# A two-layer hybrid decoder trunk on one core: the modulation weights laid transposed, their column sums formed along the row on VectorE, and the first norm's statistics with tokens on partitions

## The chip, the cores and the metric

The kernel runs on one core of a Trainium2 chip. It is one program with five engines that each work through their own list of instructions in order: PE (TensorE, matrix products; its weight loads are listed apart as PEld), DVE (VectorE), ACT (ScalarE), POOL (GpSimd) and SP (SyncE, which issues nearly all DMAs here). Engines wait for each other by semaphores. SBUF is the memory on the chip, 128 partitions wide, PSUM holds what PE writes, and weights come from HBM by DMA.

The metric is the device time of one execution in microseconds (us). The traces are of one profiled execution each, which has its own time; the other runs have no trace.

## What is computed

The input is x (512 tokens of 1024 features) and one condition vector c (1024). Two layers follow one another; each has three sub-layers, a feed-forward half step, a token mixing, and another feed-forward half step. Before each the state is normed and modulated by a shift, a scale and a gate that come from c:

```python
def rms_norm(x, gain):
    y = xf * lax.rsqrt(jnp.mean(xf * xf, axis=-1, keepdims=True) + EPS)
    return (y * gain).astype(x.dtype)

def swiglu(x, w_in, w_out):
    gate, up = jnp.split(x @ w_in, 2, axis=-1)
    return (jax.nn.silu(gate) * up) @ w_out

c_act = jax.nn.silu(c)
for l in range(DEPTH):                                    # 2
    mod = (c_act @ w_ada[l] + b_ada[l]).reshape(B, 9, 1024)
    sh1, sc1, gt1, sh2, sc2, gt2, sh3, sc3, gt3 = ...
    hn = rms_norm(h, g_ffn1[l]) * (1.0 + sc1) + sh1
    h = h + 0.5 * (1.0 + gt1) * swiglu(hn, w_ffn1_in[l], w_ffn1_out[l])
    hn = rms_norm(h, g_mix[l]) * (1.0 + sc2) + sh2
    ...                                                   # attention, RWKV-7, short convolution
    h = h + (1.0 + gt2) * mixed
    hn = rms_norm(h, g_ffn2[l]) * (1.0 + sc3) + sh3
    h = h + 0.5 * (1.0 + gt3) * swiglu(hn, w_ffn2_in[l], w_ffn2_out[l])
```

The change is about `mod`: one vector of 1024 times a matrix of 1024 x 9216 in each layer, all in float32 (37.7 MB of weights a layer, each used once). The matrices of the feed-forward steps are 1024 x 5632 and 2816 x 1024.

## The kernel before

**State and products.** The state h lies with features on partitions: eight tiles of 128 features x 512 tokens. All large products are made of three fast matmuls in a reduced format: weights and activations are each split into a high and a low part (`split`: ACT casts the high part, L89, DVE subtracts it for the low part, L90), and `mm3` issues high x high (L84), high x low (L85) and low x high (L86) into one PSUM tile `ps_mm`. One tile of a feed-forward input product is 8 pieces of the inner dimension x 3 = 24 matmuls of 128x512.

**Weights.** `load_w` brings 128x1024 floats (512 KB) into `wraw` (two buffers) by a DMA on SP and splits them into `wH` and `wL` (four buffers each), so weights can be ready up to four tiles ahead. The order of instructions on each engine is fixed when the program is built; a scheduler may pull instructions ahead of where the code issues them, as far as their buffers are free.

**Modulation in the body.** `todo` lists the half vectors (layer, one of nine, half) of 512 outputs. A step (`ada_step`) forms one of them: eight DMAs of 256 KB bring 128 rows each of `w_ada` (`wada`, three buffers), and DVE multiplies each by the silu of c on its partition and adds them up (`ada_add`: first L145, then seven times L147), giving a 128x512 tile whose columns must still be summed over the partitions. That sum is closed in the next step (`ada_close`): the tile is split into `ada_h` and `ada_l` (L89, L90), two matmuls with a matrix of ones (L174, L175) put the total on every partition, and DVE multiplies by an identity (L177), reduces along the row (L179) and adds the bias (L164). The half vector then lies as four columns of `mod`, features on partitions, which is how the norms use it. 32 of these steps run in three feed-forward stages: 13 in the first of layer 0 (`ffn1`), 7 in the second of layer 0 (`ffn2`), 12 in the first of layer 1. `ada_until` makes sure that what the next sub-layer needs is done.

**The start (`begin`).** The first shift and scale can't be hidden behind anything, so they are made in four groups, each for two tiles of 128 features. The DMAs on SP are, in order: c, the eight tiles of x, the parameters `par`, 2 x 1 MB of modulation weights for group 0 (`wada`), two first weight tiles (`wfirst`), group 1, two more weight tiles, groups 2 and 3, then the constants `con`. For each group DVE sums five of the eight row blocks (`sums_vec`), PE takes three in plain float32 matmuls with one output row (`sums_ten`, L892), and one more matmul with ones joins both (`sums_end`, L895); ACT copies the row out (L897), four tiny matmuls lay it onto partitions (`modulate`, L903), and DVE adds bias and gain (L905, L906). Meanwhile ACT squares x (L207, L210), DVE adds the squares (L211), one matmul with ones gives the sum of squares of each token on all partitions (L931), ACT takes the root (L933), and DVE the reciprocal of the 128x512 tile (L934). `normed` then multiplies h by it (L910), modulates on ACT (L912) and splits. The first four weight tiles are consumed group by group, so PE works on a group as soon as its two normed tiles are there. 72 matmuls of ones (L925) run before.

**Between stages.** While the last output tile of a stage is still being computed, in two halves of 256 tokens, `then` prepares the next norm by halves: `stats` (sum of squares L224, Sqrt on ACT L226, reciprocal on DVE L227) and `apply` (DVE L234, ACT L235, DVE L236). ACT keeps one set of function tables at a time; going from Silu to Sqrt and back loads a table.

Of the kernel before, what the change touches and what calls it, by code (L numbers as in the profile page):

```python
# [14 lines left out]
P = 128  # L15
# [38 lines left out]
def trunk_kernel(ctx, tc, ins, out, layers=L, phases=("ffn1", "mix", "ffn2")):  # L54
# [85 lines left out]
    mod = {}  # L140

    def ada_add(acc, w, k, first):
        c = cact[:, k : k + 1]
        if first:
            ts(acc, w, c, None, ALU.mult)  # L145
        else:
            stt(acc, w, c, acc, ALU.mult, ALU.add)  # L147

    def ada_sum(pool, l, i, hf):

        src = ins["w_ada"][l].rearrange("(k p) n -> p k n", p=P)
        n0 = i * D + hf * 512
# [7 lines left out]
    def ada_put(l, i, hf, v):  # L160
# [3 lines left out]
        tt(mod[l, i][:, hf * 4 : hf * 4 + 4], v, prm(l, "b_ada")[:, c0 : c0 + 4], ALU.add)  # L164

    todo = [(l, i, hf) for l in range(layers) for i in range(9) for hf in range(2)]
    open_ = []

    def ada_close():
        if open_:  # L170
            key, aH, aL = open_.pop()
            pt = psum([P, 4, P], "ps_ada")
            f = pt.rearrange("p a b -> p (a b)")
            mm(f, ones_r, aH, start=True, stop=False)  # L174
            mm(f, ones_r, aL, start=False, stop=True)  # L175
# [6 lines left out]
    def ada_step(pool):  # L182
        ada_close()
        if todo:
            key = todo.pop(0)
            acc = ada_sum(pool, *key)
            aH = pool.tile([P, T], F32R, name="ada_h", tag="ada", bufs=2)
            aL = pool.tile([P, T], F32R, name="ada_l", tag="ada", bufs=2)
            split(aH, aL, acc)
            open_.append((key, aH, aL))  # L190

    def ada_until(pool, l, i):
        while todo and todo[0] <= (l, i, 1):
            ada_step(pool)
        if open_ and open_[0][0] <= (l, i, 1):
            ada_close()
# [78 lines left out]
    def ffn(l, w_in, w_out, hn, im, ss, ada, need, then, first=None):  # L275
        with tc.tile_pool(name="act", bufs=2 * NF) as ap_:
            xs = []
            tiles = (t for t in projector([w_in[l, j, g] for j in range(NF) for g in range(2)], hn, BANKS[:3], first) if t is not None)
            for j in range(NF):
# [7 lines left out]
                if j in ada:  # L287
                    ada_step(ap_)
            ada_until(ap_, l, im + 2)
# [8 lines left out]
            for i in range(KD - 1):  # L298
# [5 lines left out]
                if NF + i in ada:  # L304
                    ada_step(ap_)
            last = list(pieces(KD - 1))
            ada_until(ap_, *need)
            ada_close()
# [542 lines left out]
    def begin(pool):  # L851
        hn = [tuple(hnp.tile([P, T], F32R, name=n, tag="hn") for n in ("hnH", "hnL")) for _ in range(KD)]
        m0 = const.tile([P, 2, KD], F32, name="mod0_01")
        for i in range(2):
            mod[0, i] = m0[:, i]
            for hf in range(2):
                todo.remove((0, i, hf))
        bias = prm(0, "b_ada")[:, : 2 * KD].rearrange("p (i k) -> p i k", k=KD)
        gm = small_.tile([P, KD], F32, name="gmod", tag="gmod")
        wa, wf, ws = {}, [], []  # L860

        def fetch(m):
            for k0 in (0, 4):
                w = pool.tile([P, 4, 512], F32, name="wada", tag="wada", bufs=8)
                nc.sync.dma_start(w, ins["wa0"][m, :, k0 : k0 + 4])
                for k in range(4):
                    wa[m, k0 + k] = w[:, k]
# [12 lines left out]
        VEC, TEN = (0, 1, 2, 4, 5), (3, 6, 7)  # L880
        acc, row = {}, {}

        def sums_vec(m):
            acc[m] = pool.tile([P, T], F32, name="ada_acc", tag="ada_acc", bufs=2)
            for k in VEC:
                ada_add(acc[m], wa[m, k], k, k == VEC[0])

        def sums_ten(m, ks):
            if m not in row:
                row[m] = psum([1, T], "ps_row")  # L890
            for k in ks:
                mm(row[m], cact[:, k : k + 1], wa[m, k], start=k == TEN[0], stop=False)  # L892

        def sums_end(m):
            mm(row[m], ones[:, :1], acc[m], start=False, stop=True)  # L895
            r = pool.tile([1, T], F32, name="ada_row", tag="ada_row", bufs=2)
            nc.scalar.copy(r, row[m])  # L897
            row[m] = r

        def modulate(m):  # L900
            pt = psum([P, 2, 2], "ps_ada")
            for n in range(4):
                mm(pt[:, n // 2, n % 2 : n % 2 + 1], row[m][:, n * P : (n + 1) * P], ones[:1, :1], start=True, stop=True)  # L903
# [173 lines left out]
```

## Time and profile before

| | us |
|---|---|
| three runs | 2064.97, 2067.78, 2068.11 |
| their median | 2067.78 |
| the profiled execution | 2066.95 |
| its span, first to last instruction | 2065.2 |
| mean granted TensorE clock in it | 0.995 of full |

The page of the profile also says what was moved: 252.31 MB of DMA, among it 256 transfers of 256 KB for `wada` in the body, 8 of 1 MB at the start, and 280 `wraw` transfers of 512 KB.

How to read the lines: a row of the page or of a view that groups instructions has the source line, the engine, the operation, output<-inputs, shapes, the count, then "| busy us, mean ns | idle time of the engine just before them, and what ended it". A row of the timeline has the start and the duration in us, the engine, the line and the operation; neighbours of the same kind are drawn together with their count, and in brackets stands how long the engine had been idle and what it waited for ("<-"). Matmuls overlap in the pipeline, so their rate is read from the distance of their starts, not from their duration. SPq rows are DMA issues, and their duration includes waiting for a buffer.

### The profile page before, as it was taken

Reading aid. Unit: us, or ns where it says so; the run is one execution under the profiler, and the core shown is the slowest. Engines: PE = TensorE matmul, PEld = TensorE weight load, DVE = VectorE, ACT = ScalarE, POOL = GpSimd, SP = SyncE. Lnnn points to the kernel's source line nnn. Section 1 sums busy time; section 2 is a strip of 40 time slices with the busy share of each in tenths; the row PEclk is TensorE's granted clock in tenths of the full one; section 3 lists DMA queues with packets and bytes.
Section 4 is the critical chain, followed back from the end, with each engine's and each line's share of the span. In section 5 each row is a group of like instructions: output and inputs, shape, how many; then the busy total and the mean of one; then the engine's idle time right before and its main releaser. Section 6 shows DMA issues by size and latency. Waiting matters only on the chain.

```text
span 2065.2 us, 27744 instructions
## 1 busy us (share of the span) xinstructions
PE 2031.5 (98%) x11194; PEld 1651.0 (80%) x11194; DVE 1164.7 (56%) x1833; ACT 672.2 (33%) x1044; POOL 3.9 (0%) x16
## 2 busy tenths in 40 slices
PE   9999999999999999999999999999999999999999
PEld 5788888886677888888888888888767778888888
DVE  6656665567875834554374666555577664333321
ACT  4423322246322432232243223223553233323211
POOL 0000000000000000000000000000000000000000
PEclk9999999999999999999999999999999999999999
DMA  6556555331222534453344666532212123333332
GB/s 277 189 154 193 184 170 182 102 95 31 57 63 72 173 103 135 141 160 117 112 130 144 190 194 185 176 120 72 82 41 62 54 72 90 94 100 94 100 110 67
DMA packets 102705, 252.31 MB, mean 122 GB/s; under 512 B 23216, under 2 KB 24112, under 8 KB 101552
## 3 DMA queue, kind: packets, MB, share of 16 engines
q1 hardware_dynamic: 102576, 250.53, 39.0%
q8 instruction: 88, 1.44, 0.3%
q14 instruction: 41, 0.34, 0.0%
HBM read 247.08 MB, written 3.41 MB: 121 GB/s over the span
## 4 chain that ended last, share of the span: by engine, by line
PE 88%; DVE 8%; ACT 2%; issue 1%; DMA 1%; SPq 0%; DVEq 0%; ACTq 0%
PE ps_mm L84 27%; PE ps_mm L85 26%; PE ps_mm L86 26%; DVE wL L90 1%; PE ps_av L777 1%; PE ps_sc L731 1%; PE ps_warm L925 1%; PE ps_c L537 1%; DVE rn L506 1%; DVE iP L505 1%; DVE rstd L227 1%; PE ps_row L892 0%; ACT wH L89 0%; PE ps_ada L174 0%; DVE inv L565 0%
## 5 line engine op out<-in xcount | busy, mean ns | idle before, releaser
L84 PE MATMUL ps_mm<-hnH,wH 128*128 128x512 f32 (+1 forms) x1848 | 697.2, 381 | 15.1 <-ACT hnH L235 12.5
L85 PE MATMUL ps_mm<-hnL,wH 128*128 128x512 f32 (+1 forms) x1848 | 702.4, 381 | 0.2
L86 PE MATMUL ps_mm<-hnH,wL 128*128 128x512 f32 (+1 forms) x1848 | 698.1, 379 | 1.1 <-DVE wL L90 1.1
L89 ACT CAST wH<-wraw 128x1024 fp32r<-128x1024 f32 (+1 forms) x328 | 334.4, 1021 | 1079.3 <-PE ps_mm L85 702.8
L90 DVE TENSOR_TENSOR wL<-wraw,wH 128x1024 fp32r<-128x1024 f32 (+1 forms) x328 | 387.2, 1181 | 400.5 <-ACT wH L89 392.7
L84 PEld LDWEIGHTS ps_mm<-hnH,wH 128*128 128x128 f32 x1848 | 347.1, 190 | 89.0 <-ACT hnH L235 15.2
L85 PEld LDWEIGHTS ps_mm<-hnL,wH 128*128 128x128 f32 x1848 | 350.5, 190 | 70.7 <-issue 5.1
L86 PEld LDWEIGHTS ps_mm<-hnH,wL 128*128 128x128 f32 x1848 | 350.4, 190 | 69.2 <-issue 4.8
L84 PE MATMUL ps_mm<-actH,wH 128*128 128x512 f32 (+1 forms) x792 | 290.1, 366 | 0.0
L86 PE MATMUL ps_mm<-actH,wL 128*128 128x512 f32 (+1 forms) x792 | 289.7, 366 | 0.0
L85 PE MATMUL ps_mm<-actL,wH 128*128 128x512 f32 (+1 forms) x792 | 289.6, 366 | 0.0
L147 DVE SCALAR_TENSOR_TENSOR ada_acc<-wada,cact,ada_acc 128x512 f32<-128x512 f32 x240 | 179.7, 749 | 37.9 <-DMA wada<-in_w_ada 32.2
L283 DVE TENSOR_TENSOR silu<-silu,ps_mm 128x512 f32<-128x512 f32 x88 | 60.3, 687 | 213.6 <-PE ps_mm L86 208.5
L85 PEld LDWEIGHTS ps_mm<-actL,wH 128*128 128x128 f32 x792 | 149.4, 189 | 24.6
L84 PEld LDWEIGHTS ps_mm<-actH,wH 128*128 128x128 f32 x792 | 149.4, 189 | 24.4
L86 PEld LDWEIGHTS ps_mm<-actH,wL 128*128 128x128 f32 x792 | 149.4, 189 | 24.2
L272 DVE SCALAR_TENSOR_TENSOR h<-ps_mm,cg,h 128x512 f32<-128x512 f32 (+1 forms) x36 | 24.9, 691 | 83.7 <-PE ps_mm L86 83.7
L90 DVE TENSOR_TENSOR actL<-silu,actH 128x512 fp32r<-128x512 f32 x88 | 60.1, 683 | 0.0
L89 ACT CAST actH<-silu 128x512 fp32r<-128x512 f32 x88 | 54.5, 620 | 5.1 <-DVE silu L283 5.1
L282 ACT ACTIVATE silu<-ps_mm 128x512 f32<-128x512 f32 x88 | 51.2, 586 | 2.0 <-PE ps_mm L86 2.0
L235 ACT ACTIVATE hnH<-hn_t,mod 128x256 fp32r<-128x256 f32 x80 | 36.3, 501 | 37.5 <-DVE hn_t L234 37.4
L210 ACT ACTIVATE sq<-h 128x512 f32<-128x512 f32 (+1 forms) x49 | 27.4, 567 | 32.5 <-DVE h L272 28.9
(289 smaller groups left out, 1531.5 us busy)
## 6 DMA issues: line engine op xcount, KB each, us to landing
wada<-in_w_ada SPq DMA_DIRECT2D x256, 256.0 KB
wraw<-in_w2i SPq DMA_DIRECT2D x88, 512.0 KB
wraw<-in_w1i SPq DMA_DIRECT2D x84, 512.0 KB
wraw<-in_wmi SPq DMA_DIRECT2D x40, 512.0 KB
wraw<-in_w1o SPq DMA_DIRECT2D x32, 512.0 KB
wraw<-in_w2o SPq DMA_DIRECT2D x32, 512.0 KB
wada<-in_wa SPq DMA_DIRECT2D x8, 1024.0 KB
wraw<-in_w1o SPq DMA_DIRECT2D x16, 384.0 KB
```

Of the source, the lines that this page charges most:

```text
L84: mm(acc, wH, xH, start=start, stop=False)
L85: mm(acc, wH, xL, start=False, stop=False)
L86: mm(acc, wL, xH, start=False, stop=stop)
L89: nc.scalar.copy(hi, src)
L90: nc.vector.tensor_sub(lo, src, hi.bitcast(F32))
L147: stt(acc, w, c, acc, ALU.mult, ALU.add)
L210: act(sq[:, sl], h[i][:, sl], AF.Square)
L227: nc.vector.reciprocal(r, r)
L235: act(a, t, AF.Identity, bias=sh)
L272: stt(h[i][:, sl], pt, gate[:, i : i + 1], h[i][:, sl], ALU.mult, ALU.add)
L282: act(s, pg, AF.Silu)
L283: tt(s, s, pu, ALU.mult)
```

## The change

**In the body.** The weights lie transposed: a row of `wadaT` has on partition p all 1024 inputs of output p. With silu(c) copied onto every partition (`crep`, 128x1024), one DVE instruction multiplies a 128x1024 weight tile by it and writes the sum along the row to one column of `mod`, through the accumulator output (`ada_dot`); the product overwrites the weights. A step is now four DMAs of 512 KB (two buffers), four such dots and one bias addition. The split, the two matmuls, the masking product and the reduction are gone, and with them `ada_close`. `crep` is loaded and its Silu taken again in each feed-forward stage that still has steps to run, out of that stage's own pool (three times).

**At the start.** `crep` is fetched ahead of the modulation weights, and the constants' first 128 columns (the identity) behind those of group 0. A group's weights hold two columns of scale, one of shift, transposed, and the second shift column in the old orientation: DVE forms the first three by dots, PE the fourth by eight matmuls with one column. The statistics are made with tokens on partitions: four matmuls with one output column each, Sqrt and reciprocal on a 128x4 tile, and four matmuls with the identity, whose stationary operand is the broadcast column, put rstd back over all partitions, into PSUM. The warm-up has 36 matmuls instead of 72. The rest of `con` is fetched after group 3.

In the scheduled order of the changed program, DVE has two dots behind each weight tile from the start of a feed-forward stage, and SP two `wada` transfers behind each `wraw`, until the stage's steps are used up.

```diff
-    def ada_add(acc, w, k, first):
...
-    def ada_sum(pool, l, i, hf):
-        acc = pool.tile([P, T], F32, name="ada_acc", tag="ada_acc", bufs=1)
-        for k in range(KD):
-            w = pool.tile([P, 512], F32, name="wada", tag="wada", bufs=3)
-            nc.sync.dma_start(w, src[:, k, n0 : n0 + 512])
-            ada_add(acc, w, k, k == 0)
-        return acc
...
-    def ada_close():
-        if open_:
-            key, aH, aL = open_.pop()
-            pt = psum([P, 4, P], "ps_ada")
-            f = pt.rearrange("p a b -> p (a b)")
-            mm(f, ones_r, aH, start=True, stop=False)
-            mm(f, ones_r, aL, start=False, stop=True)
-            d = E("ada_d").rearrange("p (a b) -> p a b", b=P)
-            tt(d, pt, rep("ident", 4), ALU.mult)
-            red = small_.tile([P, 4], F32, name="ada_red", tag="ada_red")
-            nc.vector.tensor_reduce(red, d, AXL.X, ALU.add)
-            ada_put(*key, red)
...
+    todo = [(l, i, hf) for l in range(layers) for i in range(9) for hf in range(2)][4:]
+
+    def ada_dot(out_, w, crep):
+        stt(w, w, 1.0, crep, ALU.mult, ALU.mult, accum_out=out_)
+
+    def ada_crep(pool):
+        c = pool.tile([P, D], F32, name="crep", tag="crep", bufs=1)
+        nc.sync.dma_start(c, ins["crep"])
+        act(c, c, AF.Silu)
+        return c
+
+    def ada_step(pool, crep):
+        if not todo:
+            return
+        l, i, hf = todo.pop(0)
         if (l, i) not in mod:
             mod[l, i] = const.tile([P, KD], F32, name=f"mod{l}_{i}")
+        for k in range(4 * hf, 4 * hf + 4):
+            w = pool.tile([P, D], F32, name="wada", tag="wada", bufs=2)
+            nc.sync.dma_start(w, ins["wadaT"][l, i, k])
+            ada_dot(mod[l, i][:, k : k + 1], w, crep)
+        m = mod[l, i][:, 4 * hf : 4 * hf + 4]
         c0 = i * 8 + hf * 4
+        tt(m, m, prm(l, "b_ada")[:, c0 : c0 + 4], ALU.add)
...
     def ffn(l, w_in, w_out, hn, im, ss, ada, need, then, first=None):
             xs = []
+            crep = ada_crep(ap_) if todo else None
...
     def begin(pool):
...
+            for n in (0, 2):
+                w = pool.tile([P, 2, D], F32, name="wada", tag="wada", bufs=8)
+                nc.sync.dma_start(w, ins["wa0"][m, :, n : n + 2])
...
+        def scales(m):
+            for n in range(2):
+                k = slice(2 * m + n, 2 * m + n + 1)
+                ada_dot(col["sc"][:, k], wa[m, n], crep)
+                stt(col["gm0"][:, k], col["sc"][:, k], g1[:, k], col["gb"][:, k], ALU.mult, ALU.add)
+
+        def shifts(m):
+            k0, k1 = (slice(2 * m + n, 2 * m + n + 1) for n in range(2))
+            ada_dot(col["sh"][:, k0], wa[m, 2], crep)
+            tt(col["sh0"][:, k0], col["sh"][:, k0], bsh[:, k0], ALU.add)
+            pt = psum([P, 1], "ps_ada")
+            for k in range(KD):
+                mm(pt, wa[m, 3][:, k * P : (k + 1) * P], cact[:, k : k + 1], start=k == 0, stop=k == KD - 1)
+            tt(col["sh0"][:, k1], pt, bsh[:, k1], ALU.add)
...
+        crep = ada_crep(pool)
         fetch(0)
+        nc.sync.dma_start(con[:, :P], ins["con"][:, :P])
         fetch_w()
         fetch_w()
         fetch(1)
...
-        for _ in range(72):
+        for _ in range(36):
             mm(pw, ones_r, ones_r, start=True, stop=True)
...
-        pt = psum([P, T], "ps_ss")
-        mm(pt, ones, ss, start=True, stop=True)
-        rstd = pool.tile([P, T], F32, name="rstd0", tag="rstd0")
-        act(rstd, pt, AF.Sqrt, bias=vals["eps"], scale=1.0 / D)
-        nc.vector.reciprocal(rstd, rstd)
-        sums_ten(0, TEN)
-        sums_end(0)
-        modulate(0)
+        pt = psum([P, NB], "ps_ss")
+        for b in range(NB):
+            mm(pt[:, b : b + 1], ss[:, b * P : (b + 1) * P], ones[:, :1], start=True, stop=True)
+        r = pool.tile([P, NB], F32, name="rstd_t", tag="rstd_t")
+        act(r, pt, AF.Sqrt, bias=vals["eps"], scale=1.0 / D)
+        nc.vector.reciprocal(r, r)
+        rstd = psum([P, T], "ps_rstd", "r0")
+        for b in range(NB):
+            mm(rstd[:, b * P : (b + 1) * P], r[:, b : b + 1].to_broadcast([P, P]), cst("ident"), start=True, stop=True)
+        scales(0)
+        shifts(0)
...
             for g, (n, k) in enumerate(groups):
                 mm3(pts[n], ws[n], k, hn[k], ALL, k == 0, k == KD - 1)
-                if m < 3:
-                    if g == 0:
-                        sums_vec(m + 1)
-                        sums_ten(m + 1, TEN[:1])
...
+                if m < 3 and g == 1:
+                    scales(m + 1)
+                    shifts(m + 1)
+                    if m == 0:
+                        split_w(2)
+                        split_w(3)
+                    normed(2 * m + 2)
+                    normed(2 * m + 3)
```

More of the change, by code (lines that the diff above doesn't have):

```diff
@@ L304, in ffn @@
                 if NF + i in ada:
-                    ada_step(ap_)
+                    ada_step(ap_, crep)
             last = list(pieces(KD - 1))
-            ada_until(ap_, *need)
-            ada_close()
+            ada_until(ap_, crep, *need)
             half = then()
@@ L878, in split_w @@
             ws.append(pair)
[L880 to L903, printed above, removed]
-            ks = slice(2 * m, 2 * m + 2)
-            tt(m0[:, :, ks], pt, bias[:, :, ks], ALU.add)
-            stt(gm[:, ks], m0[:, 1, ks], 1.0, prm(0, "g1")[:, ks], ALU.add, ALU.mult)
+        def scales(m):
[11 more added lines that the diff above has]
+            tt(col["sh0"][:, k1], pt, bsh[:, k1], ALU.add)
         def normed(k):
```

71 lines of the change are left out of this document (16 added, 55 removed).

## The prediction

> **What bounds the kernel now.** I read first the busy times and the chain of waits of the page, then windows cut where the stages begin.
>
> ```profile
> PE 2031.5 (98%) x11194; PEld 1651.0 (80%) x11194; DVE 1164.7 (56%) x1833; ACT 672.2 (33%) x1044; POOL 3.9 (0%) x16
> PE 88%; DVE 8%; ACT 2%; issue 1%; DMA 1%; SPq 0%; DVEq 0%; ACTq 0%
> ```
>
> ```profile
> 0.00:64.00 64.00, 58.71 (x219) 36.20 (x220) 38.06 (x64) 26.73 (x39) 0.21 (x4) 1.00 0.60 235
> 64.00:406.00 342.00, 342.00 (x1541) 283.99 (x1540) 208.63 (x283) 101.90 (x131) 0.00 (x0) 1.00 0.56 175
> 680.00:694.00 14.00, 11.81 (x79) 11.24 (x80) 13.46 (x27) 6.11 (x14) 0.00 (x0) 0.88 0.32 103
> 694.00:1043.00 349.00, 349.00 (x1608) 291.68 (x1607) 167.47 (x218) 100.81 (x130) 0.00 (x0) 1.00 0.43 132
> 1043.00:1066.00 23.00, 20.12 (x146) 18.87 (x145) 19.63 (x37) 11.58 (x21) 0.00 (x0) 0.95 0.43 138
> 1066.00:1419.00 353.00, 353.00 (x1625) 294.92 (x1624) 203.23 (x275) 102.71 (x134) 0.00 (x0) 1.00 0.52 161
> ```
>
> In a window row stand the stretch, its length, then PE, weight loads, DVE, ACT and POOL, each busy us (x instructions), the granted clock, the DMA share and GB/s. In three stretches, 64 to 406, 694 to 1043 and 1066 to 1419, PE has no gap at all: they are the three FFN stages in which the 32 modulation steps run. There a matmul taken away is time taken away, whatever DVE does, as long as DVE (203 to 209 of about 350 us) and the weight loads stay in front. Only the start (0 to 64) and the short changes of stage are set by something else.
>
> **PE work removed.** Each step closes with two 128x512 matmuls, which the new code doesn't have.
>
> ```profile
> L174 PE MATMUL ps_ada<-ada_h,ones_r x32: 404/404/505, 121.8 to 1407.0; 128*128 128x512 f32 x32
> L175 PE MATMUL ps_ada<-ada_l,ones_r x32: 402/402/442, 122.1 to 1407.3; 128*128 128x512 f32 x32
> ```
>
> ```profile
> 65.62 0.39 PE L84 MATMUL ps_mm<-hnH,wH 128*128 128x512 f32 x1
> ...
> 69.93 0.39 PE L86 MATMUL ps_mm<-hnH,wL 128*128 128x512 f32 x1
> ```
>
> Records last 0.40 us but overlap: these two rows are the first and last of 20 in a row, 19 starts in 4.31 us, 0.227 us each. 64 x 0.227 = **14.5 us**, all between 121 and 1408 us, in the saturated stretches. At most it would be 64 x 0.28 us = 18 if a matmul with another weight source cost half a step more; at least 12 if a few fell into gaps.
>
> **The new VectorE work: does it still hide?** Eight passes over 128x512, a split, a masking product and a reduction per step become four fused dots over 128x1024.
>
> ```profile
> L90 DVE TENSOR_TENSOR wL<-wraw,wH 128x1024 fp32r<-128x1024 f32 x280 | 341.4, 1220 | 298.3 <-ACT wH L89 290.5
> L147 DVE SCALAR_TENSOR_TENSOR ada_acc<-wada,cact,ada_acc 128x512 f32<-128x512 f32 x240 | 179.7, 749 | 37.9 <-DMA wada<-in_w_ada 32.2 <-DMA wada<-in_wa 0.5 <-DVE ada_acc L147 0.2
> L90 DVE TENSOR_TENSOR actL<-silu,actH 128x512 fp32r<-128x512 f32 x88 | 60.1, 683 | 0.0
> L234 DVE SCALAR_TENSOR_TENSOR hn_t<-h,gmod,rstd 128x256 f32<-128x256 f32 x80 | 35.1, 477 | 0.0
> ```
>
> ```profile
> L748 ACT ACTIVATION_READ_ACCUMULATOR Sc<-Sc,mx,rq x64: 185/187/191, 464.7 to 1532.0; 128x1 f32 x64
> ```
>
> The operation with three inputs grows by (749 - 477)/256 = 1.06 ns an element, so 1024 elements take 1.29 us. The dot also reads out its accumulator, which no DVE row shows; the nearest is ScalarE's, 0.187 us. Bounds: 1.29 (readout free) and 1.69 (two 512-wide passes and that readout). I take 1.40, nearer to the one-instruction row.
>
> The Trainium skill, "Vector Engine (DVE) Microarchitecture Reference", section "Points that are easy to get wrong", speaks against the change: this instruction with two sources in SBUF that aren't bf16 runs at half throughput, both read ports being used and none left for accumulator readback. The 1.06 ns of this trace, without an accumulator, isn't half of anything the trace shows; with one, no row tells. By that page it would be the rival "slow dot" below.
>
> In the scheduled order of the changed program the steps have moved forward: from the start of an FFN stage, two dots follow each weight tile on DVE and two modulation DMAs each weight DMA on SP. PE needs 24 x 0.227 = 5.45 us a tile, 10.9 us for two. DVE's load for two: 2 x 1.22 (low parts) + 0.68 (activation's) + 0.69 (silu product, the same form) + 0.15 + 4 x 1.40 = 9.6 us. It fits up to a dot of about 1.7 us. The transfers: with two buffers, two dots per tile need one landing, one dot and some 0.1 us.
>
> ```profile
> 94.65 1.05 ACT L89 CAST wH<-wraw 128x1024 fp32r<-128x1024 f32 x1 [2.80 <-PE ps_mm L85]
> ```
>
> ```profile
> 1049.41 0.33 SPq L246 DMA_DIRECT2D wraw<-in_w1i  x1
> ...
> 1053.06 1.05 ACT L89 CAST wH<-wraw 128x1024 fp32r<-128x1024 f32 x1 [0.36 <-DMA wraw<-in_w1i]
> ```
>
> A 512 KB transfer took 3.65 us from issue to use, so the loop is 3.65 + 1.40 + 0.1 = 5.15 us, under 5.45. And ACT's casts wait for PE to free a weight buffer, not for data: with four buffers about three tiles (16 us) are ready ahead, so a loop of up to 5.45 + 16/26 = 6.1 us over the 26 tiles of 13 steps would still hide. Price here: 0.
>
> **The start.**
>
> ```profile
> 2.38 15.62 PE L925 MATMUL ps_warm<-ones_r 128*128 128x128 f32 x72 [2.38 <-ACT ones_r L113]
> 10.41 0.69 DVE L211 TENSOR_TENSOR ss<-ss,sq 128x512 f32<-128x512 f32 x1
> 12.30 0.49 DVE L145 TENSOR_SCALAR ada_acc<-wada,cact 128x512 f32<-128x512 f32 x1 [1.19 <-DMA wada<-in_wa]
> 14.82 1.54 DVE L147 SCALAR_TENSOR_TENSOR ada_acc<-wada,cact,ada_acc 128x512 f32<-128x512 f32 x2 [0.46 <-DMA wada<-in_wa]
> 16.02 1.04 ACT L89 CAST wH<-wfirst 128x1024 fp32r<-128x1024 f32 x1 [6.00 <-DMA wfirst<-in_w1i]
> 18.31 1.28 ACT L933 ACT_TABLE_LOAD   x1
> 20.56 0.13 PEld L892 LDWEIGHTS ps_row<-wada,cact 128*1 128x1 f32 x1 [0.72 <-issue]
> 20.57 3.35 DVE L934 RECIPROCAL rstd<-rstd 128x512 f32<-128x512 f32 x1 [1.02 <-ACT rstd L933]
> 21.41 0.13 PEld L892 LDWEIGHTS ps_row<-wada,cact 128*1 128x1 f32 x1 [0.73 <-issue]
> ...
> 26.82 0.08 PEld L892 LDWEIGHTS ps_row<-wada,cact 128*1 128x1 f32 x1 [0.35 <-issue]
> 27.18 0.15 DVE L906 SCALAR_TENSOR_TENSOR gmod<-mod,par 128x2 f32<-128x2 f32 x1
> 27.25 0.08 PEld L892 LDWEIGHTS ps_row<-wada,cact 128*1 128x1 f32 x1 [0.34 <-issue]
> 27.43 0.81 ACT L912 ACTIVATE hn_t<-z,mod,gmod 128x512 f32<-128x512 f32 x1 [2.06 <-DVE gmod L906]
> 29.08 0.61 ACT L89 CAST hnH<-hn_t 128x512 fp32r<-128x512 f32 x1
> 29.75 0.96 PE L84 MATMUL ps_mm<-hnH,wH 128*128 128x512 f32 x3 [0.62 <-ACT hnH L89]
> ...
> 61.82 1.21 PE L84 MATMUL ps_mm<-hnH,wH 128*128 128x512 f32 x4 [0.93 <-ACT hnH L89]
> ```
>
> The last of the four groups of the first stage starts at 61.82 us; from there PE is full. What sets that instant after the change? Of data, 1 MB arrives in 14.82 - 12.30 = 2.5 us, 512 KB in 1.2. The replicated condition goes ahead, so it lands near 11 and the first megabytes near 13.4 and 16. Half of the warm-up ends at 10.2 (2.38 + 7.8), the squares' sum at 11.1: the statistics no longer wait for the warm-up's end at 18. They cost four small matmuls, a table load (1.28) and a reciprocal on four columns; then ACT loads the Silu table again (1.28) and applies it to 128x1024 (1.05), which frees the dots at about 15.9. First group: three dots (4.2) and four small operations (0.15 each), to 20.7; the product with rstd (0.68), modulation (0.81), another cast on ACT (1.05) and its own cast (0.61): first matmul at about 24 instead of 29.75. From there DVE is the bound. A group is 4.2 + 0.6 + 2 x 0.68 + 2 x 0.68 = 7.5 us, and the four first weight tiles add 4.9. So the dots of groups two, three and four end near 31, 41 and 49 (weights and normed tiles of the group before lie between them), the last operands are cast at about 52, and the last group starts there: 61.8 - 52.1 = **9.7 us** gained. With 12 dots in the chain it is 11 at a dot of 1.29 and 6.2 at 1.69. The shifts' eight one-column matmuls a group, each at most the 0.43 us between the last 512-wide row sums shown, take 3.4 us beside DVE's dots.
>
> **The changes of stage.** The replicated vector is loaded and activated again in three FFN stages, and dots stand among the norms.
>
> ```profile
> 676.47 0.74 DVE L147 SCALAR_TENSOR_TENSOR ada_acc<-wada,cact,ada_acc 128x512 f32<-128x512 f32 x1
> 677.40 1.75 DVE L227 RECIPROCAL rstd<-rstd 128x256 f32<-128x256 f32 x1 [0.20 <-ACT rstd L226]
> 680.45 0.62 PE L84 MATMUL ps_mm<-hnH,wH 128*128 128x256 f32 x3 [1.62 <-ACT hnH L235]
> ```
>
> Here PE waits for a normed tile behind the reciprocal. In the new order two dots (2.8) stand where one pass (0.74) stood: **+2.1 us** (0 if they run before the statistics arrive; 4.1 if the second pair shows too). The matching place at 1043 to 1066 gets one dot ahead of the second half's norm and, on ACT, a Silu table load, the Silu and a Sqrt table load between the casts: 1.40 + 1.28 of the 5.0 us show, I take **+2.6** (0 to 5). In the first FFN stage the load of the vector waits for the last normed tile of the start, and ACT's Silu stands ahead of a weight cast; three tiles are ready by then: 0.
>
> **Sum**, against the profiled run's 2066.95 us (span 2065.2 and 1.75 around it; 0.8 under the median): 2066.95 - 14.5 - 9.7 + 2.1 + 2.6 = **2047.4 us**. With the bounds: 2066.95 - 18 - 11 = 2038, and 2066.95 - 12 - 6.2 + 9.1 = 2058.
>
> **Rivals.**
>
> *Cold start.* Weight loads of the row sums follow each other by 0.85 us (20.56, 21.41) and later by 0.43 (26.82, 27.25): PE began at half speed, and 72 short warm-up matmuls hadn't changed that; only the dense 512-wide ones did. The new start has half the warm-up, and one-column matmuls instead of those. If the clock stays down through the first groups, 24 matmuls take 24 x 2 x 0.227 = 10.9 us, more than DVE's 7.5: the last group starts at 24 + 3 x 10.9 = 56.7 and itself takes up to 5.4 more. Nothing is left of the start's gain: 2066.95 - 14.5 + 4.7 = **2057**. Against it: before the change the pace doubled between 21.41 and 26.82, after few matmuls. The Trainium skill, "TensorE: Matmul & The Clock Gate", section "What's actually happening", puts the release after one busy window of about 3.4 us and the throttle after an idle one, so waits on DVE between groups could throttle it again; the two paces agree with its half rate.
>
> *The gain is hidden or spent elsewhere*: the start ends as before, because a chain through ACT (two table loads, the Silu, casts) takes the place of DVE's, and the stage changes cost their upper 9.1: 2066.95 - 14.5 + 9.1 = **2061.5**. For it: ACT has three switches of table at the start. Against: ACT was busy 27 of 64 us.
>
> *Slow dot*, on the other side: the fused dot with accumulator runs at half rate, 2 x 1.06 x 1.024 + 0.2 = 2.4 us. DVE's two-tile load becomes 13.6 against 10.9 us. Over 13, 7 and 12 steps the lag is 35, 19 and 32 us, less 16 of lead each: 19 + 3 + 16 = 38 us of starved PE, and the start's 12 dots add 12: 2047.4 + 50 = **2097**. It decides from a dot of about 1.7 us, and the lead is used up at 2.05. For it: no row shows a DVE accumulator.
>
> *Starved queue*: SP holds weight loads behind modulation loads that wait for a buffer. At a loop of 7 us the lag is 26 x 1.55 - 16 = 24, 24 x 1.55 - 16 = 21 and 14 x 1.55 - 16 = 6: **2098**. It decides at 6.1; the measured 3.65 us landing would have to be 5.5. Bandwidth doesn't speak for it: 1.5 MB in 5.45 us is 275 GB/s, and the start moves 1 MB in 2.5 us.
>
> **How the numbers follow.** Forecast 0.56, cold start 0.18, hidden or spent 0.11, slow dot 0.10, starved queue 0.05. Forecast's own range 2038 to 2058. The slower 0.15 can be left out, with little at the low end: 2038 to 2064. About 0.2% (4 us) is what a measurement here tells from no change. Faster holds the forecast, the cold start and half of hidden: 0.79; same, the rest of hidden: 0.06; slower 0.15.
>
> **What would show it.** Right: no matmuls of ps_ada after the start; DVE's dots near 1.40 us with their readout; PE full in the three FFN stretches, each shorter by 0.454 us a step; ps_mm's first row near 24 us and the last start group near 52; longer PE gaps at the two stage changes. Wrong: dots over 1.7 us; casts of wH in the FFN stages waiting for wraw instead of PE; low-clock rows past 30 us; the last start group at 58 or later.

## The result, and the profile after

| | before | after |
|---|---|---|
| median, us | 2067.61 (4 runs, 2064.97 to 2068.11) | 2042.39 (4 runs, 2039.83 to 2043.98) |
| profiled execution, us | 2066.95 | 2039.83 |
| its span, us | 2065.2 | 2038.0 |
| mean granted clock in it | 0.995 | 0.995 |

The ratio is 0.9879, interval 0.9862 to 0.9897: 25 us faster, between 21 and 28.5. A second series of the changed kernel gave a median of 2041.69 and 0.9867 (0.9853 to 0.9882). The forecast was 2047.4.

The page after, busy time and chain of waits:

```profile
PE 1996.9 (98%) x11108; PEld 1639.0 (80%) x11108; DVE 1083.4 (53%) x1750; ACT 661.5 (32%) x1016; POOL 3.9 (0%) x16
PE 88%; DVE 8%; ACT 2%; DMA 1%; issue 1%; SPq 0%; DVEq 0%; ACTq 0%
```

The shape is the same: PE's work is 88% of the chain of waits. PE's busy time fell by 34.6 us, DVE's by 81. Windows of the three feed-forward stages after (columns as in the prediction):

```profile
53.40:390.00 336.60, 336.60 (x1521) 280.24 (x1520) 177.11 (x245) 94.66 (x118) 0.00 (x0) 1.00 0.57 181
680.00:1021.00 341.00, 341.00 (x1559) 284.54 (x1557) 147.78 (x192) 97.02 (x123) 0.00 (x0) 1.00 0.41 131
1046.00:1392.00 346.00, 344.67 (x1574) 288.39 (x1575) 174.65 (x245) 98.10 (x125) 0.00 (x0) 1.00 0.51 163
```

PE is still full there (the 1.33 us missing in the third lie at its very start, in the change of stage). To see where the 27 us between the two profiled executions come from, I take the same instants of both: the last start group and the first matmul of each stage. The timeline of before (its last start group at 61.82 and the first matmul of ffn2 of layer 0 at 680.45 stand in the prediction):

```profile
413.50 0.62 PE L84 MATMUL ps_mm<-hnH,wH 128*128 128x256 f32 x3 [0.31 <-ACT hnH L235]
...
1050.37 0.62 PE L84 MATMUL ps_mm<-hnH,wH 128*128 128x256 f32 x3 [0.31 <-ACT hnH L235]
...
1424.24 0.62 PE L84 MATMUL ps_mm<-hnH,wH 128*128 128x256 f32 x3 [0.31 <-ACT hnH L235]
...
1695.40 1.01 PE L84 MATMUL ps_mm<-hnH,wH 128*128 128x256 f32 x3 [2.24 <-ACT hnH L235]
```

and of after, the last start group first:

```profile
53.40 0.84 PE L84 MATMUL ps_mm<-hnH,wH 128*128 128x512 f32 x3
...
397.41 0.52 PE L84 MATMUL ps_mm<-hnH,wH 128*128 128x256 f32 x3
...
666.34 1.01 PE L84 MATMUL ps_mm<-hnH,wH 128*128 128x256 f32 x3 [3.12 <-ACT hnH L209]
...
1032.34 0.52 PE L84 MATMUL ps_mm<-hnH,wH 128*128 128x256 f32 x3
...
1401.60 0.52 PE L84 MATMUL ps_mm<-hnH,wH 128*128 128x256 f32 x3
...
1668.12 0.63 PE L84 MATMUL ps_mm<-hnH,wH 128*128 128x256 f32 x3 [2.16 <-ACT hnH L209]
```

| stretch | before | after | gained, us | steps x 0.454 |
|---|---|---|---|---|
| start, to the last start group | 61.82 | 53.40 | 8.42 | |
| ffn1 of layer 0 | 351.68 | 344.01 | 7.67 | 13: 5.90 |
| mix of layer 0, with the change to ffn2 | 266.95 | 268.93 | -1.98 | |
| ffn2 of layer 0, with its second change | 369.92 | 366.00 | 3.92 | 7: 3.18 |
| ffn1 of layer 1 | 373.87 | 369.26 | 4.61 | 12: 5.45 |
| mix of layer 1 | 271.16 | 266.52 | 4.64 | |
| ffn2 of layer 1, to the span's end | 369.80 | 369.88 | -0.08 | |

The last column is what two matmuls a step, at 0.454 us, would give. The sum of the gains is 27.2 us. One row can't be the change's: nothing in the mixing of layer 1 was altered, and it gained 4.64 us. A window of before and the same place in after show why:

```profile
1571.00:1579.00 8.00, 8.00 (x58) 6.01 (x55) 7.38 (x16) 0.59 (x1) 0.00 (x0) 0.58 0.48 110
```

```profile
1544.00:1552.00 8.00, 6.37 (x71) 4.44 (x72) 8.00 (x23) 0.00 (x0) 0.00 (x0) 1.00 0.11 29
```

At the same place of the program TensorE was granted a mean of 0.58 in one execution and full speed in the other. Windows of 1 us through all profiles show that the clock drops to half for 3.4 us, or twice or three times that, mostly at stage changes and in the mixings. The changed kernel has such stretches where the kernel before has fewer or none; two windows of after:

```profile
645.00:648.00 3.00, 3.00 (x9) 2.35 (x8) 0.69 (x1) 0.21 (x1) 0.00 (x0) 0.50 0.57 165
666.00:672.00 6.00, 5.66 (x26) 5.66 (x27) 6.00 (x15) 3.44 (x9) 0.00 (x0) 0.50 0.47 160
```

The first lies in the mixing of layer 0 and takes part in the loss of that row; the second is part of a stretch of 6.8 us, where before has one of 3.4 at that place. So the row of layer 1's mixing can't be taken out alone. Over the whole span both executions stood at half clock for the same 20.5 us; behind the start it is 20.5 us before and 17.1 after. If half of that time is lost, an estimate, the stretches make 1.7 of the 27.2 us, and 25.5 are left. Runs of the second series with the same mean clock, 0.994, took 2067.9 to 2068.9 us before and 2041.2 and 2042.0 after, 26 to 28 us apart; the medians say 25 to 27.

### The profile page after: what moved, and what is told of

The parts are those of the page before. It is cut to its first block, busy times and chain, and to the rows that moved or that the text cites. A ratio compares the mean times of both kernels' runs of the same rounds, so it can differ in the third digit from the quotient of the medians.

```text
span 2038.0 us, 27002 instructions
## 1 busy us (share of the span) xinstructions
PE 1996.9 (98%) x11108; PEld 1639.0 (80%) x11108; DVE 1083.4 (53%) x1750; ACT 661.5 (32%) x1016; POOL 3.9 (0%) x16
## 4 chain that ended last, share of the span: by engine, by line
PE 88%; DVE 8%; ACT 2%; DMA 1%; issue 1%; SPq 0%; DVEq 0%; ACTq 0%
PE ps_mm L84 27%; PE ps_mm L85 27%; PE ps_mm L86 27%; DVE wL L90 1%; PE ps_av L751 1%; PE ps_sc L705 1%; DVE rn L480 1%; DVE iP L479 1%; ACT wH L89 1%; DMA wada<-in_wa 0%; PE ps_c L511 0%; DVE hn_t L208 0%; PE ps_ada L862 0%; DVE rstd L201 0%; DMA wraw<-in_w2i 0%
## 5 line engine op out<-in xcount | busy, mean ns | idle before, releaser
L84 PE MATMUL ps_mm<-hnH,wH 128*128 128x512 f32 (+1 forms) x1848 | 696.2, 381 | 17.9 <-ACT hnH L209 12.9
L145 DVE SCALAR_TENSOR_TENSOR wada<-wada,crep 128x1024 f32<-128x1024 f32 x140 | 170.7, 1223 | 82.6 <-DMA wada<-in_wadaT 80.1
L210 DVE SCALAR_TENSOR_TENSOR hnL<-hn_t,mod,hnH 128x256 fp32r<-128x256 f32 x80 | 36.2, 478 | 0.8 <-ACT hnH L209 0.4
```

Of the source, the lines that this page charges most:

```text
L84: mm(acc, wH, xH, start=start, stop=False)
L145: stt(w, w, 1.0, crep, ALU.mult, ALU.mult, accum_out=out_)
L210: stt(b, t, sh, a.bitcast(F32), ALU.add, ALU.subtract)
```

## The experiments

Every time is a median beside runs of the kernel before on the same chip; that kernel's median was 2067.4 to 2068.9 in the three series. Where few us matter I read the profile at the places named, since half-clock stretches scatter whole runs by some us.

### Putting the matmuls back: free, and tied to their step

`e1_pe_back` adds to every body step of the changed kernel two matmuls that nobody reads (`wide` is the matrix of ones, read four times over):

```diff
             ada_dot(mod[l, i][:, k : k + 1], w, crep)
+        pt = psum([P, 4, P], "ps_ada")
+        for n in range(2):
+            mm(pt, ones_r, wide, start=n == 0, stop=n == 1)
```

> The changed kernel with two 128x512 matmuls of ones put back into each of the 32 body steps, into a PSUM tile that nobody reads; DVE, ACT and the DMAs stay as after the change. Theory (the body's gain is PE time, 64 starts of 0.227 to 0.24 us each): 14.5 to 15.4 us over the changed kernel's 2042.4, so about 2057. Rival (the gain came from DVE's shorter load or from fewer DMAs): 2042 to 2045.

Measured: 2051.25 us (ratio 0.9915, 0.9894 to 0.9936), 9 us more: between the two theories. The timeline of that kernel says why:

```profile
685.89 2.46 PE L167 MATMUL ps_ada<-ones_r 128*128 128x512 f32 x10
...
1053.93 3.59 PE L167 MATMUL ps_ada<-ones_r 128*128 128x512 f32 x15
```

Ten of them stand in a row at the beginning of ffn2 of layer 0 and fifteen at the beginning of ffn1 of layer 1. They depend on nothing, so the scheduler issued them early, into the changes of stage, where PE has gaps: its waits for a normed tile from ACT add up to 8.6 us in this kernel, and to 12.9 in the changed one. So `e1b_pe_tied` ties them to the step's last product:

```diff
+        x = pool.tile([P, 2 * P], F32R, name="xcopy", tag="xcopy", bufs=1)
+        nc.scalar.copy(x, w[:, : 2 * P])
+        pt = psum([P, 2, 2 * P], "ps_ada")
+        for n in range(2):
+            mm(pt, ones_r, x.unsqueeze(1).to_broadcast([P, 2, 2 * P]), start=n == 0, stop=n == 1)
```

> The changed kernel with two 128x512 matmuls put back into each body step, this time reading a copy (128x256, made by ACT, read twice over) of the step's last product, so that they can't be issued ahead of the step and fall into the gaps at the stage changes, as the free ones did. Theory (64 starts of 0.227 us in saturated stretches): 14.5 us over the changed kernel, 2056 to 2058. Rival (the free matmuls' 9 us is the whole worth, and the rest of the body's gain is from another place): 2050 to 2052.

Measured: 2058.06 us (0.994, 0.9923 to 0.9957), 16.4 over the changed kernel's 2041.69 in the same series. Its timeline at the last start group and at the first matmul of the mixing:

```profile
51.41 1.07 PE L84 MATMUL ps_mm<-hnH,wH 128*128 128x512 f32 x4
...
401.31 0.52 PE L84 MATMUL ps_mm<-hnH,wH 128*128 128x256 f32 x3
```

From the one to the other are 349.90 us, against 344.01 in the changed kernel: 5.89 us for 13 steps, 0.453 each, where the prediction had 2 x 0.227. No half-clock stretch lies between the two instants. The theory that the body's gain is PE time holds; only the free form of the test failed.

### The two halves of the change, alone

`e2_new_start` is the kernel before with the whole new `begin` (its weights, its `crep`, its DMA order); `e3_old_start` the changed kernel with the old one. Core of the first:

```diff
-    todo = [(l, i, hf) for l in range(layers) for i in range(9) for hf in range(2)]
+    todo = [(l, i, hf) for l in range(layers) for i in range(9) for hf in range(2)][4:]
...
+        crep = ada_crep(pool)
         fetch(0)
+        nc.sync.dma_start(con[:, :P], ins["con"][:, :P])
```

> The kernel before with the new start alone; all 32 body steps as before. Theory (the start's gain stands by itself, last start group at 53.4 instead of 61.8 us): 2067.6 - 8.4 = 2059. Rival (what the start wins is lost again behind it, where weights or modulation come late): 2065 to 2068.

> The changed kernel with the old start; the body steps as after the change. Theory (the two parts add up): 2042.4 + 8.4 = 2051. Rival (the body's part is worth less or more than 14.5 to 16.5 by itself): under 2047 or over 2055.

Measured: the new start alone 2055.37 us (0.994, 0.9922 to 0.9959), 12 us faster than before with an interval of 8.5 to 16; the new body alone 2050.14 (0.9909, 0.9882 to 0.9936), 17 us faster (13 to 24). Both parts stand by themselves, and their sum, 29, is the whole gain of 25 to 27 within these intervals. No loss behind the start takes the start's gain back. The new start alone gave 3.6 us more than the 8.4 forecast from its place in the profile; the runs' mean clock, 0.992 to 0.997, scatters by that much.

### The slow dot

`e7_dots_twice` does each body dot twice on the same tile:

```diff
             ada_dot(mod[l, i][:, k : k + 1], w, crep)
+            ada_dot(again, w, crep)
```

> The changed kernel with every body dot done twice on the same weight tile, the second sum going to a scratch column (the second one multiplies the product again). DVE's load for two weight tiles rises from 2.44 + 0.69 + 0.69 + 0.15 + 4 x 1.15 = 8.6 to 13.2 us against PE's 10.9. Prediction's mechanism of the slow dot: lags of 13 x 2.3 = 30, 7 x 2.3 = 16 and 12 x 2.3 = 28 us less 16 of lead each, so 26 us more: 2068. Rival (DVE's average over a whole stage counts, and it has room enough): 2042 to 2046.

Measured: 2051.67 us (0.992, 0.9892 to 0.9947), 9 us more, where 26 was priced. In windows of the dots' line alone (DVE busy, instructions with a readout for each dot), the changed kernel first, then this one:

```profile
54.00:94.00 40.00, 13.89 (x23) 1.00 0.86 286
...
174.00:214.00 40.00, 17.26 (x28) 1.00 0.79 261
214.00:254.00 40.00, 0.00 (x0) 1.00 0.42 128
```

```profile
54.00:94.00 40.00, 19.62 (x33) 1.00 0.74 227
...
214.00:254.00 40.00, 24.65 (x41) 1.00 0.75 227
254.00:294.00 40.00, 9.39 (x16) 1.00 0.52 158
```

The 52 dots of the changed kernel are done by 214 us, 14 in 40 us. The 104 here go on to about 270, 20 in 40 us: not four for each weight tile, as I had assumed, but 2.7. Between 54 and 400 us PE waits only for this:

```profile
PE ps_mm L86 <- DVE wL L90: 3.8, 5, 2.1
```

In DVE's own order of that stretch mostly three dots, at times two or four, follow a weight tile, where the changed kernel has two (one behind each of the first six tiles). So the scheduler, which reckons with how long an instruction takes, spread the longer work over more tiles. The price of this rival rested on an order that I took to be fixed. The 9 us aren't all DVE's: in the whole span PE's waits for low parts are 5.3 us against 1.6, its waits for normed tiles from ACT 15.6 against 12.9, and these runs had a mean clock of 0.991 to 0.993.

### The starved queue

`e8_one_buffer`: `bufs=1` for `wada` in the body instead of 2.

> The changed kernel with one buffer instead of two for the body's modulation weights. A dot then needs a landing (3.65 us), itself (1.15) and 0.1: 4.9 us, two of them 9.8 us a weight tile on SP's queue against PE's 5.45. Prediction's mechanism of the starved queue: 26, 14 and 24 tiles of 4.35 us lag each, less 16 of lead: 97 + 45 + 88 = 230 us more, 2270. Rival (the scheduled order spreads the transfers when buffers are short, or SP has room): under 2100.

Measured: 2044.43 us (0.9886, 0.9867 to 0.9904): 2 us over the changed kernel, not 230. Two windows of its dots:

```profile
294.00:334.00 40.00, 9.87 (x16) 1.00 0.67 200
334.00:374.00 40.00, 0.00 (x0) 1.00 0.33 95
```

and DVE's wait for them in the whole span:

```profile
DVE wada L145 <- DMA wada<-in_wadaT: 188.2, 115, 4.2
```

DVE waits over twice as long for these transfers as with two buffers (80.1 us), and it costs nothing: with one buffer the order has one transfer and one dot to a weight tile, 52 in 280 us, done 56 us before the stage ends. The 4.9 us of landing and dot fit beside one tile's 5.45.

### The start: warm-up, clock, fourth column

`e5_warm72` puts the 72 warm-up matmuls back, `e6_dense_fill` adds dense ones behind the statistics, `e9_col_dve` takes the columns from PE:

```diff
-        for _ in range(36):
+        for _ in range(72):
```

```diff
+        pd = psum([P, T], "ps_dense", "mm")
+        for _ in range(3):
+            mm(pd, ones, ss, start=True, stop=True)
...
+        for _ in range(3):
+            mm(pd, r[:, :1].to_broadcast([P, P]), ss, start=True, stop=True)
```

```diff
-            for k in range(KD):
-                mm(pt, wa[m, 3][:, k * P : (k + 1) * P], cact[:, k : k + 1], start=k == 0, stop=k == KD - 1)
-            tt(col["sh0"][:, k1], pt, bsh[:, k1], ALU.add)
+            ada_dot(col["sh"][:, k1], wa[m, 3], crep)
+            tt(col["sh0"][:, k1], col["sh"][:, k1], bsh[:, k1], ALU.add)
...
```

> The changed kernel with 72 warm-up matmuls as before. Theory (the start's gain hangs on the statistics not waiting for the warm-up: ACT's Silu of the replicated vector stands behind the Sqrt, and all dots behind it): the sums start at 18 instead of 11.2, the dots at 22.5 instead of 15.75, last start group 5 to 7 us later, 2047 to 2049. Rival (longer warm-up brings the clock up sooner and pays for itself): 2041 to 2044.

> The changed kernel with three plain float32 512-wide matmuls behind the statistics' sums and three behind the reciprocal, into an unread PSUM tile, to keep PE dense between 13 and 18 us. Theory (the granted clock stayed low until about 37 us after the change, and that costs): the pace of the first group's matmuls is 0.23 instead of 0.43 us from about 25 us on, last start group about 2 us earlier, at 51 to 52, 2040 to 2041. Rival A (DVE sets the start, the pace doesn't matter): last start group at 53 to 54, 2042 to 2043. Rival B (the fill only delays the column matmuls behind it): 2043 to 2045.

> The changed kernel with the fourth column of each start group also formed by a DVE dot (its weights transposed too), so that the eight one-column matmuls a group are gone from PE. Theory (DVE waited 1.4 and 2.1 us for those matmuls and rstd stood behind them): first matmul of the first group 0.5 to 1 us earlier, last start group 1 to 2 us earlier, 2040 to 2041.5. Rival (12 dots were the bound, 16 are worse): 1 to 3 us later, 2043 to 2045.

With 72: 2041.19 us (0.9862, 0.9845 to 0.9878), no difference; my theory fell. Its timeline:

```profile
11.94 1.06 ACT L150 ACTIVATE crep<-crep 128x1024 f32<-128x1024 f32 x1 [0.93 <-DMA crep<-in_crep]
...
14.50 1.23 DVE L145 SCALAR_TENSOR_TENSOR wada<-wada,crep 128x1024 f32<-128x1024 f32 x1 [2.30 <-DMA wada<-in_wa]
...
17.81 1.81 PE L892 MATMUL ps_ss<-ones_r,ss 128*128 128x1 f32 x8
```

The sums do start 6.6 us later, but with them late the scheduler put ACT's Silu ahead of the Sqrt. The dots start 1.25 us earlier than in the changed kernel, as soon as their weights land. The first matmul is 3 us later (27.78), the last start group 0.5 (53.94). This profile has no half-clock stretch in the start; beside the two profiles of the unaltered start without one (51.41 in `e1b_pe_tied`, 51.73 in `e7_dots_twice`) it is 2.2 to 2.5 later, which the median doesn't show. So in the changed kernel a longer warm-up costs far less than the 5 to 7 us of the theory; what the old kernel's own wait for it cost, no run tells.

With the dense fill: 2046.11 us (0.9889, 0.9865 to 0.9913), last start group at 56.67, worse. The fill did raise the clock (its first six matmul records took 4.61 us, the next six 2.74), and it didn't hold:

```profile
21.55 1.84 PE L862 MATMUL ps_ada<-cact,wada 128*128 128x1 f32 x16
...
29.46 0.63 PE L86 MATMUL ps_mm<-hnH,wL 128*128 128x512 f32 x1
29.89 0.63 PE L85 MATMUL ps_mm<-hnL,wH 128*128 128x512 f32 x1
```

The columns took 1.84 us instead of 3.54, but PE then idled for 3 us before its first product, and that ran at 0.43 us a matmul again. The windows have half clock from 25 to 32 us and from 35 to 42.

With the fourth column on DVE: 2042.26 us (0.9873, 0.9854 to 0.9892), the median unmoved, but the place that the edit touches did move:

```profile
16.25 2.05 PE L896 MATMUL ps_rstd<-con,rstd_t 128*128 128x128 f32 x8 [3.03 <-DMA con<-in_con]
...
50.78 1.20 PE L84 MATMUL ps_mm<-hnH,wH 128*128 128x512 f32 x4 [1.07 <-ACT hnH L89]
```

rstd starts 3.4 us earlier, and the last start group begins at 50.78, 2.6 us earlier, both profiles having one half-clock stretch in the start. With the start unaltered that instant lies between 51.41 and 54.96 in the other profiles, so the 2.6 are not clear of the scatter; `e12_kept_dve` with this edit (51.97) lies 3.0 before `e4_crep_kept` without it (54.96). The mean clock of these four runs was 0.991 to 0.993, of the changed kernel's eight 0.992 to 0.995.

### Keeping silu(c), and both edits together

`e4_crep_kept` stores the activated `crep` to HBM once and reloads it; `e12_kept_dve` is this and the fourth column on DVE.

```diff
+        if kept:
+            nc.sync.dma_start(c, kept[0])
+            return c
         nc.sync.dma_start(c, ins["crep"])
         act(c, c, AF.Silu)
+        kept.append(dram.tile([P, D], F32, name="crep_d"))
...
+        nc.sync.dma_start(kept[0], crep)
```

> The changed kernel with silu(c) on all partitions written to HBM once at the start and reloaded from there in the three stages, so that ACT's three Silu passes over 128x1024 and their table loads are gone from the stages. Prediction's step (the stage change at 1021 to 1046 pays 1.3 us for a table load): 1 to 2 us less, 2040.5 to 2041.5. Rival (they lie beside other work): 2042 to 2043.

> The changed kernel with both edits that seemed to help: the fourth start column by a DVE dot, and silu(c) reloaded from HBM instead of activated again. Theory (both gains add: 2.6 us at the start, some 3.5 at the change to the second layer): 2035 to 2038. Rival (the single runs differed by where the half-clock stretches fell): 2040 to 2043.

Measured: 2037.46 us (0.985, 0.9833 to 0.9868) for the first, 2040.96 (0.9861, 0.9846 to 0.9876) for both, against 0.9867 (0.9853 to 0.9882) for the changed kernel. In the first, the second half's norm at the change to layer 1 comes sooner:

```profile
1047.12 0.86 PE L84 MATMUL ps_mm<-hnH,wH 128*128 128x256 f32 x4 [2.33 <-ACT hnH L215]
```

PE's waits in this change add up to 2.9 us (0.56 and 2.33) instead of 4.57. That gives the edit 1.7 us, and its median 4 to 5, three of its four runs having a clock of 0.996. Both edits together stand at 2038.8 at a clock of 0.994, where the changed kernel's two runs at 0.994 stand at 2041.2 and 2042.0: some 3 us, not enough to be told apart in medians. No version here beats the changed kernel beyond doubt.

## Why the prediction was right, step by step

**PE work removed: right, a little small.** 14.5 us was forecast, and the tied matmuls cost 0.453 us a step, as priced. The old steps cost slightly more than that. In the timeline of before, around one of them:

```profile
121.84 0.40 PE L174 MATMUL ps_ada<-ada_h,ones_r 128*128 128x512 f32 x1
122.08 0.40 PE L175 MATMUL ps_ada<-ada_l,ones_r 128*128 128x512 f32 x1
```

Around each of the eleven steps of the first stage that lie among 512-wide matmuls, six starts lie 0.231 to 0.242 us apart instead of 0.227, so a step cost about 0.51: 16.3 us in all. Why they are slower, no run tells; the pair itself isn't enough, for in `e1b_pe_tied` the pairs stand among starts of 0.227. The 0.31 us that PE waited ahead of three stages (the rows at 413.50, 1050.37 and 1424.24) are gone, too: ACT now loads the Sqrt table before the sum of squares is there, not after it. That change in the order of ACT's work wasn't foreseen.

**The dot: mis-sized, by the step that extrapolated it.** 1.40 us was taken, with 1.29 as the lower bound. The timeline:

```profile
15.75 1.23 DVE L145 SCALAR_TENSOR_TENSOR wada<-wada,crep 128x1024 f32<-128x1024 f32 x1 [2.19 <-ACT crep L150]
...
16.90 0.08 DVE L145 DVE_READ_ACCUMULATOR wada<-wada,crep 128x1 f32 x1
16.90 1.22 DVE L145 SCALAR_TENSOR_TENSOR wada<-wada,crep 128x1024 f32<-128x1024 f32 x1
```

Dots follow each other by 1.15 us, readout included, less than the 1.29 that I had called a bound; the record itself is 1.22 to 1.23. The line drawn through two other forms, 256 and 512 elements without an accumulator, didn't carry to this one. The readout is a DVE instruction of its own, 0.08 us, beside the next dot's beginning. The rule of the Trainium skill weighed in the prediction ("Vector Engine (DVE) Microarchitecture Reference", "Points that are easy to get wrong": half throughput) would by the prediction's working have made this 2.4 us; the trace disagrees, 1.12 ns an element with both sources in SBUF, in float32 and accumulating, against 1.06 by the prediction's rows without an accumulator.

**The start: 9.7 forecast, 8.4 measured, by two errors that offset each other.** With dots of 1.15 us the forecast's own working would give 12 x 0.25 = 3 us more. What it missed are PE's columns:

```profile
16.27 3.54 PE L862 MATMUL ps_ada<-cact,wada 128*128 128x1 f32 x16 [3.22 <-DMA wada<-in_wa]
...
19.67 2.05 PE L898 MATMUL ps_rstd<-con,rstd_t 128*128 128x128 f32 x8
21.76 1.28 DVE L867 TENSOR_TENSOR z<-h,ps_rstd 128x512 f32<-128x512 f32 x2 [1.69 <-PE ps_rstd L898]
...
24.87 1.22 PE L84 MATMUL ps_mm<-hnH,wH 128*128 128x512 f32 x2 [3.14 <-ACT hnH L89]
...
32.48 0.16 DVE L863 TENSOR_TENSOR sh<-ps_ada,par 128x1 f32<-128x1 f32 x1 [1.44 <-PE ps_ada L862]
...
43.31 0.16 DVE L863 TENSOR_TENSOR sh<-ps_ada,par 128x1 f32<-128x1 f32 x1 [2.06 <-PE ps_ada L862]
```

"Beside DVE's dots" was wrong. rstd stands behind the columns on PE, and the columns of the next groups stand behind the products: DVE idles 1.69, 1.44 and 2.06 us for them, 5.2 together. `e9_col_dve` took them away and won some 2.6. So the step "from there DVE is the bound" was wrong: DVE and PE held each other up. That 8.4 came so near to 9.7 is luck.

**Cold start: it came, at a part of its price.** PE's first group ran at 0.43 us a matmul until about 30 us. The granted clock doesn't show it: its windows read 1.00 until 33 us. From 30.6 to 33 us PE ran at full pace (16 column records in 1.84 us), and then came a half-clock stretch, granted 0.50 from 34 to 37, in the second group:

```profile
35.14 0.63 PE L86 MATMUL ps_mm<-hnH,wL 128*128 128x512 f32 x1
35.56 0.63 PE L85 MATMUL ps_mm<-hnL,wH 128*128 128x512 f32 x1
```

From 37.56 on they are 0.23 apart. It didn't last through three groups, so most of the start's gain stayed; what that stretch cost shows in `e1b_pe_tied`, whose start is unaltered: its first matmul starts at the same 24.87, its clock stays up, and its last start group begins at 51.41 instead of 53.40, 2 us earlier (51.73 in `e7_dots_twice`, also without the stretch). So the start's gain is 8.4 with the stretch and about 10 without. What the half pace up to 30 us cost, no run isolates, since the dense fill that raised the clock also delayed the columns. The Trainium skill's "TensorE: Matmul & The Clock Gate", section "What's actually happening", has a window of about 3.4 us, two states and a throttle after an idle window. The traces agree on the first two, the stretches being 3.4 us or a multiple of it at a granted 0.5. On the third they don't: in `e1b_pe_tied` the clock fell to half at 448.8 us, in the mixing of layer 0, while PE was busy without a gap:

```profile
447.00:448.00 1.00, 1.00 (x7) 0.64 (x7) 0.97 (x3) 0.00 (x0) 0.00 (x0) 1.00 0.76 303
...
449.00:450.00 1.00, 1.00 (x4) 0.72 (x4) 1.00 (x5) 0.00 (x0) 0.00 (x0) 0.50 0.00 0
```

What ran there, from 445.06 to 448.64, were 24 matmuls of 2 and 128 columns and one of 512.

**The changes of stage: right place, half the price.** At the change to ffn2, PE's two waits grew from 1.62 and 1.71 us to 3.12 and 1.27, 1.1 instead of the forecast 2.1. At the change to layer 1 they grew from 2.85 in all to 4.57, 1.7 instead of 2.6. The dot that was to stand ahead of the second half's norm is there:

```profile
1045.10 1.23 DVE L145 SCALAR_TENSOR_TENSOR wada<-wada,crep 128x1024 f32<-128x1024 f32 x1 [0.69 <-DMA wada<-in_wadaT]
...
1046.25 1.27 DVE L208 SCALAR_TENSOR_TENSOR hn_t<-h,gmod,rstd 128x256 f32<-128x256 f32 x3
...
1047.33 1.13 PE L84 MATMUL ps_mm<-hnH,wH 128*128 128x256 f32 x4 [3.24 <-ACT hnH L209]
```

It waits 0.69 us for its weights and takes 1.15, while the norm, ready to go, stands behind it on DVE and PE behind the norm.

**The rivals.** Hidden or spent elsewhere: the halves alone exclude it. Slow dot and starved queue: neither happened, and both were overpriced by the same mistake. I read the order of the changed program (two dots, two transfers a tile) as a given and let a longer dot or landing run against it; the order is itself made from durations and buffers, and moved with them in `e7_dots_twice` and `e8_one_buffer`. A dot slower on the chip than the scheduler believes would still meet a fixed order; that wasn't tried.

**The sum.** By the ledger of the profiles, with the steps at 0.51: 16.3 + 8.4 - 1.1 - 1.7 + 0.6 (two waits of 0.31; the third is already in the change to layer 1) = 22.5 us. The two profiles differ by about 25.5 us without the half-clock stretches behind the start, so some 3 us belong to no term here, and where they come from stays open. The forecast's own terms make 19.5 us (20.4 against the median, which lay 0.8 over the profiled run): the steps were 1.8 too low and the two waits of 0.6 not in it, the changes of stage 1.9 too dear, the start 1.3 too high. So the mechanism was right in its largest term, and the sum came near in part because errors of both signs met.

## What to carry to other kernels

On an engine that is full, price a removed instruction by the distance of starts in the stream, and look for what the instruction does to its neighbours. Before a queue order is used to price a rival, ask who made it: a scheduled order changes with durations and buffers, and an instruction put back for a test has to be tied to the data of the one it replaces. Where two engines share a preparation, write down for each what stands ahead of it in its own queue; "beside the other's work" is a claim about order, not about length.

## What the runs showed that wasn't expected

The granted clock falls to half for 3.4, 6.8 or 10.2 us at a time, mostly where PE has just waited or has narrow matmuls, and two to eight such stretches in a profile scatter the time of one and the same kernel: of the six runs of `e1b_pe_tied` two took 2052.3 and 2052.5 us at a mean clock of 0.996, and one 2061.8 at 0.990, about 1.6 us for each 0.001. A median of four runs with another mean clock is off by as much, so differences under 3 us were read at their place in the profile. And 72 matmuls of 128x128 in an unbroken row, 15.6 us before the change, did not raise the pace: the weight loads behind them lay 0.85 us apart, and 0.43 only from between 21.41 and 26.82 us on, among 512-wide matmuls (rows of the prediction). In `e6_dense_fill` the pace doubled within the first microseconds of 512-wide ones.
